# A hybrid decoder layer on one core: transposed memory and norm vectors, a reordered start, value projections inside the cross attention, moved sums

## The chip, the core and the metric

The kernel runs on one core of a Trainium2 chip. The core has a matrix engine (TensorE, PE in the profile), a vector engine (VectorE, DVE), a scalar engine (ScalarE, ACT), a general engine (GpSimd, POOL) and a sync engine (SyncE, SP) that issues most DMAs. Each engine runs its own list of instructions in order, and waits at an instruction until what it reads has been written and what it writes over has been read. TensorE writes to eight PSUM banks; the other engines evict them to SBUF. The metric is the device time of one execution in microseconds (us), as a median of runs.

## The reference

The layer takes x (1024 tokens, 1024 wide) and 256 memory tokens. With h = RMSNorm(x) it computes

```
mq, mk, mv, mi, mf, mo, dq, dk, dv, cq = split(h @ w_in)
y_m = sigmoid(mo) * headnorm(mlstm(conv_silu(mq, mk), mv, mi, mf))   # branch m, 8 chunks of 128
y_d = diff_attention(dq, dk, dv)                                     # branch d, causal
mkv = rms_norm(mem, mem_g) @ w_kv                                    # 512 keys, 1024 values
q   = rms_norm(cq per head); mk = rms_norm(mkv[:512] per head)
y_c = softmax(q @ mk.T / sqrt(128)) @ mkv[512:]                      # branch c, 4 heads
g   = sigmoid(h @ w_gate + b_gate)                                   # three gates
x  += (g_m*(y_m@w_proj_m) + g_d*(y_d@w_proj_d) + g_c*(y_c@w_proj_c)) @ w_out
x  += relu(rms_norm(x) @ w_up)**2 @ w_down
```

All inputs are fp32. The change is in the start, in branch c, and in three short places of the later stages.

## The kernel before, in words

**Arithmetic.** Each fp32 operand is cut into two parts: `split` has ScalarE write a rounded hi part (L124; with a scale per partition L128) and VectorE the rest, lo (L126, L129). Each product is then three matmuls (`mm3`, L96): hi x hi, hi x lo, lo x hi.

**Stages.** (1) `phase_x`: `consts` turns the norm vectors (loaded as 101 rows, `vraw`) into columns (`vec`) by a transpose on TensorE (L222); `mem_kv` transposes the memory (16 transposes, L277) and scales it by the norm's gain into `memT`, projects keys (`wkv[0]`), scales, norms and transposes them (L300 to L310), and projects values (`wkv[1]`, `wkv[2]`); x is normed by rows (ScalarE's Square with a running sum, GpSimd's power, VectorE's product L263) and transposed into `hT` (L101, 64 transposes in 16 groups of four). (2) `branch_c`: the cross attention. A stream of steps of three matmuls (eight query tiles of eight steps, then 64 steps of the sigmoid gates) is woven with items: `turn` (transposes of queries), `scores`, `ptr` (transposes of the softmax), `values`. Each item has the number of a step, behind which it is written. (3) `branch_m`, again a stream with items. Into it `early` puts sums: four blocks of a matrix are loaded (`es`), three or four VectorE sums are made (L1506), and the results are stored for the 7-product scheme that follows later; the sums of y_c go to `xc_d`. (4) The d phase: 32 gate steps with `h_sums` (sums of hT, tiles `hb`, stored to `hc_d`), then projections and attention of branch d. (5) `wino_gates`: the last gate by the 7-product scheme, with operands `hx` read from `hc_d` and split. (6) `branches`, the output projection and `tail` (the MLP), all by the 7-product scheme (`wino`); the inverse norms that the MLP needs are made in `rstd`: sums over partitions by TensorE (`px<-ones,ssq`), a copy `st`, GpSimd's power (L151, L152), a transpose to a row (`px<-ident,st`, L1903), a copy, a store, and a load to all partitions (`rb`).

**Order.** A scheduler places the instructions of a stage on the engines' lists. Where `pinned` is set, TensorE's instructions keep the order in which the code is written; `held` and `issue_after` put an instruction behind a named earlier one.

Of the kernel before, what the change touches and what calls it, by code (L numbers as in the profile page):

```python
# [17 lines left out]
P = 128  # L18
D = 1024
# [54 lines left out]
class Layer:  # L74
# [131 lines left out]
    def consts(self, tmp):  # L206
        nc, cp, a = self.nc, self.cp, self.a
        self.mhalf = cp.tile([P, 32], F32, name="mhalf")
# [13 lines left out]
        nc.tensor.transpose(ps[:, 0:P], raw, self.ident)  # L222
        self.vec = cp.tile([P, P], F32, name="vec")
        nc.vector.tensor_copy(self.vec, ps[:, 0:P])
# [35 lines left out]
    def norm_rows(self, src, r1, scr):  # L260

        self.scale_rows(src, r1, scr)
        self.nc.vector.tensor_scalar_mul(src, src, r1)  # L263

# [5 lines left out]
    def mem_kv(self, pool, tmp, xs, rs):  # L270
        nc, a = self.nc, self.a
        memT = tmp.tile([P, NK, 2, 256], F32R, tag="memT", name="memT")
        for k in range(0, NK, 2):
            ps = self.tp_tile()
            for i in range(2):
                for t in range(2):
                    nc.tensor.transpose(  # L277
                        ps[:, (i * 2 + t) * P : (i * 2 + t + 1) * P], xs[t][:, (k + i) * P : (k + i + 1) * P], self.ident
                    )
            for i in range(2):  # L280
                self.split(
                    memT[:, k + i, 0], memT[:, k + i, 1], ps[:, i * 256 : (i + 1) * 256],
                    self.vec[:, R_MEM + k + i : R_MEM + k + i + 1],
                )
        self.mkT = pool.tile([P, 4, 2, 256], F32R, name="mkT")
        self.mv = pool.tile([P, 2, 2, D], F32R, name="mv")

        def proj(w, t):
            ps = self.mm_tile()
            for k in range(NK):  # L290
                self.mm3(
                    ps, (memT[:, k, 0, t * P : (t + 1) * P], memT[:, k, 1, t * P : (t + 1) * P]), w[k], k == 0, k == NK - 1
                )
            return ps
# [26 lines left out]
    def phase_x(self, kv, tmp):  # L321
# [20 lines left out]
        def half(hf):  # L342
            for x in xs[4 * hf : 4 * hf + 4]:
                norm(x)
# [13 lines left out]
        for _ in gen:  # L358
            pass
# [1939 lines left out]
```

## Time and profile before

| | |
|---|---|
| three runs | 2139.06, 2137.8, 2139.04 us; median 2139.04 us |
| the profiled execution | 2138.05 us, of which the span of the instructions is 2136.2 us; mean granted clock 0.997 |
| TensorE busy | 2106.2 us, 99% |
| VectorE, ScalarE, GpSimd busy | 1559.7, 1058.3, 626.0 us |
| DMA | 335.27 MB, 157 GB/s on average |

The profile is of one execution. A row of waits reads: engine, operation, tile and line of the waiting instruction; after the arrow the engine, tile and line of what came last; then the total, the number of times and the longest. A row of the timeline reads: start, duration, engine, line, operation, what is written and read, shapes, count, and in brackets the idle time before it and who ended it. Rows of overlapping matmuls give an end that is modelled.

### The profile page before, as it was taken

The numbers are of one execution on the slowest core, as the hardware profiler recorded it, in microseconds if no ns is written. First come the engines' busy times: TensorE is split into PE (matmuls) and PEld (weight loads), VectorE is DVE, ScalarE is ACT, GpSimd is POOL, SyncE is SP. The second block draws the span as 40 slices with busy tenths as digits, with TensorE's granted clock in tenths as the row PEclk, the third lists the DMA queues.
The fourth block names the chain that finished last, engine by engine and source line by source line (L and its number), as shares of the span: only waits on it lengthen the run. The fifth ranks groups of instructions, "written<-read, shape, count | busy, mean of one in ns | idle before, by whom it ended". The sixth has DMA issues, their size and how long they took to land.

```text
span 2136.2 us, 31406 instructions
## 1 busy us (share of the span) xinstructions
PE 2106.2 (99%) x10890; PEld 1824.4 (85%) x10890; DVE 1559.7 (73%) x2956; ACT 1058.3 (50%) x2181; POOL 626.0 (29%) x756
## 2 busy tenths in 40 slices
PE   7999999999999999999999999999999999999999
PEld 5888888888899999999888888888788888888887
DVE  6644677787547777777656688975588888777698
ACT  7543365465336666666554445333335544543331
POOL 2100000000111111111023042314756677665562
PEclk9999999999999999999999999999999999999999
DMA  6115457765443333333343885755334544854443
GB/s 233 57 64 167 137 172 223 257 202 182 162 126 91 96 84 85 89 97 89 95 148 119 295 303 161 263 166 174 107 121 173 190 158 156 303 173 135 154 163 109
DMA packets 180789, 335.27 MB, mean 157 GB/s; under 512 B 17385, under 2 KB 52502, under 8 KB 178582
## 3 DMA queue, kind: packets, MB, share of 16 engines
q1 hardware_dynamic: 164694, 307.05, 44.9%
q10 hardware_dynamic: 15936, 26.22, 3.3%
q8 instruction: 86, 1.41, 0.3%
q14 instruction: 73, 0.60, 0.1%
HBM read 213.62 MB, written 94.41 MB: 144 GB/s over the span
## 4 chain that ended last, share of the span: by engine, by line
PE 85%; DVE 5%; DMA 5%; ACT 3%; POOL 1%; issue 1%; SPq 0%; ACTq 0%; DVEq 0%; POOLq 0%
PE mm L96 35%; PE p L96 27%; PE mm L1725 10%; PE sc L96 5%; PE po L96 3%; PE tp L101 3%; DMA ngb<-g_dng 1%; DVE w L126 1%; DMA raw<-in_wkv 1%; PE pr L101 1%; DVE es L1506 1%; DVE cv L686 1%; DMA es<-in_wq 0%; ACT w L124 0%; DMA es<-y 0%
## 5 line engine op out<-in xcount | busy, mean ns | idle before, releaser
L96 PE MATMUL mm<-w,hT 128*128 128x384 f32 (+3 forms) x2496 | 469.4, 331 | 0.8 <-DVE dsg L129 0.7
L96 PE MATMUL mm<-hT,w 128*128 128x512 f32 x1680 | 409.7, 395 | 0.6 <-ACT gt L511 0.6
L96 PEld LDWEIGHTS mm<-w,hT 128*128 128x128 f32 x2496 | 388.7, 189 | 11.7 <-DVE dsg L129 0.9
L96 PEld LDWEIGHTS mm<-hT,w 128*128 128x128 f32 x1680 | 309.4, 189 | 61.3 <-ACT gt L511 1.0
L96 PE MATMUL p<-xo,wo 128*128 128x512 f32 x1344 | 308.4, 392 | 0.0
L96 PE MATMUL p<-xd,wo 128*128 128x512 f32 x1344 | 305.2, 389 | 0.3 <-DVE acc L69 0.3
L96 PEld LDWEIGHTS p<-xo,wo 128*128 128x128 f32 x1344 | 253.8, 189 | 53.6 <-DVE u L69 0.9
L96 PEld LDWEIGHTS p<-xd,wo 128*128 128x128 f32 x1344 | 252.1, 188 | 53.2 <-DVE acc L69 0.7
L117 ACT CAST wo<-wraw 128x896 fp32r<-128x896 f32 x121 | 114.2, 945 | 232.5 <-POOL wraw L1325 88.5
L1725 PE MATMUL mm<-xs,w 128*128 128x512 f32 x1008 | 228.6, 389 | 0.0
L1725 PEld LDWEIGHTS mm<-xs,w 128*128 128x128 f32 x1008 | 189.2, 188 | 39.3
L69 DVE TENSOR_TENSOR wo<-wraw,wo 128x896 fp32r<-128x896 f32 x124 | 150.5, 1224 | 49.1 <-ACT wo L117 49.1
L1322 POOL TENSOR_TENSOR wraw<-wraw 128x128 f32<-128x128 f32 x128 | 101.9, 796 | 196.9 <-DMA wraw<-in_wdown 99.6
L1055 ACT ACTIVATE dpe<-sc,dst,drr 128x256 f32<-128x256 f32 (+7 forms) x128 | 106.6, 833 | 96.9 <-DVE dst L1051 96.4
L126 DVE TENSOR_TENSOR w<-raw,w 128x256 fp32r<-128x256 f32 (+4 forms) x257 | 128.2, 525 | 33.4 <-ACT w L124 32.3
L124 ACT CAST w<-raw 128x256 fp32r<-128x256 f32 (+4 forms) x257 | 116.7, 488 | 41.6 <-PE mm L96 15.0
L151 POOL TENSOR_SCALAR hss<-hss 128x4 f32<-128x4 f32 x8 | 6.2, 774 | 415.0 <-ACT mscr L795 415.0
L1047 DVE CUSTOM_DVE_ANT_0 sc<-sc,tmask 128x256 f32<-128x256 f32 (+7 forms) x128 | 97.1, 759 | 13.4 <-PE sc L96 12.6
L1324 POOL TENSOR_TENSOR wraw<-wraw 128x128 f32<-128x128 f32 x128 | 95.3, 744 | 0.0
L151 POOL TENSOR_SCALAR drr<-drr 128x16 f32<-128x16 f32 x16 | 3.3, 204 | 309.6 <-DVE drr L1002 290.6
L96 PE MATMUL sc<-dk,dq 128*128 128x512 f32 (+3 forms) x384 | 91.9, 347 | 0.0
L1325 POOL TENSOR_TENSOR wraw<-wraw 128x128 f32<-128x128 f32 x128 | 88.0, 687 | 9.9
(330 smaller groups left out, 3456.5 us busy)
## 6 DMA issues: line engine op xcount, KB each, us to landing
dk<-dsg SPq DMA_DIRECT2D x64, 256.0 KB, 4.2
wraw<-in_wup SPq DMA_DIRECT2D x64, 256.0 KB, 3.2
r_d<-xts SPq DMA_DIRECT2D x16, 1024.0 KB, 4.7
wraw<-in_wdown SPq DMA_DIRECT2D x64, 256.0 KB, 3.0
wh<-es SPq DMA_DIRECT2D x56, 256.0 KB, 2.5
w<-wh SPq DMA_DIRECT2D x28, 512.0 KB, 4.3
raw<-in_wd SPq DMA_DIRECT2D x32, 384.0 KB, 3.3
gl<-gates SPq DMA_DIRECT2D x48, 256.0 KB, 4.4
```

Source lines behind the costliest of these rows:

```text
L69: return self.tc.keep_in_program_order(f(*a, **k))
L96: ins = self.nc.tensor.matmul(out, l, r, start=start, stop=stop)
L101: self.pin(self.nc.tensor.transpose(out, x, self.ident))
L117: self.cast = self.A.copy(hi, src).ins
L124: a = nc.scalar.copy(hi, src)
L126: return a, nc.vector.tensor_sub(lo, src, f32(hi))
L1047: V.tensor_tensor_reduce(out=sc[:, 0:n], in0=sc[:, 0:n], in1=self.tmask[:, D - n : D], scale=1.0, scalar=-3.0e38, op0=ALU.add, op1=ALU.max ...
L1055: nc.scalar.activation(pe[c][:, 0:n], sc[:, 0:n], AF.Exp, bias=t8[:, 2 + c : 3 + c], scale=rr[:, i, c : c + 1], accum_out=t8[:, 4 + c : 5 ...
L1322: G.tensor_add(r[:, 4], r[:, 0], r[:, 3])
L1324: G.tensor_sub(r[:, 6], r[:, 1], r[:, 0])
L1325: G.tensor_sub(r[:, 7], r[:, 2], r[:, 5])
L1725: nc.tensor.matmul(cur[u], w[:, l, c], x[:, m], start=first and i == 0, stop=last and i == 2, skip_group_check=True)
```

## The change

The host lays out the norm vectors (`vecs`) and the memory (`memT`) transposed. `vec` is loaded as it is (128 rows of 404 bytes), and the memory's split reads the loaded tile. The memory is still loaded untransposed as well, for its row norms.

`phase_x` is pinned and written anew: keys first, weight piece by weight piece and for both token tiles; then query tiles 0 and 1 woven with the transposes of x; the norms of the second half of x, the rows' norm of the memory and the key norm behind them (the keys are scaled after projection); query tiles 2 and 3 woven with the second half's transposes. In `branch_c` the stream is query tiles 4 to 7 (32 steps), the value projections (32 steps) and 64 gate steps; the value weights are loaded and split in eight pieces (`cut`) inside it. The items have other step numbers, and the pool of the softmax tiles 5 buffers for 8.

In `early` the sums of y_c for the last two of four block pairs are gone; `h_sums` makes them from whole rows (`hb`) in the d phase. In `wino_gates` the second half of the first operand's split (q = 4) is held behind the first evictions. In `wino` the table of places at which `first` takes its next step (here `rstd`'s) changes.

```diff
 def consts(self, tmp):
+        self.vec = cp.tile([P, P], F32, name="vec")
+        nc.sync.dma_start(self.vec[:, 0:R_END], a["vecs"])
...
-        raw = tmp.tile([P, P], F32, tag="vraw", name="vraw")
-        nc.vector.memset(raw, 0.0)
-        nc.sync.dma_start(raw[0:R_END, :], a["vecs"])
-        ps = self.tp_tile()
-        nc.tensor.transpose(ps[:, 0:P], raw, self.ident)
-        self.vec = cp.tile([P, P], F32, name="vec")
-        nc.vector.tensor_copy(self.vec, ps[:, 0:P])
...
 def phase_x(self, kv, tmp):
+        for i in range(4):
+            nc.sync.dma_start(memr[:, 2 * i : 2 * i + 2], a["memT"][:, 2 * i : 2 * i + 2])
+            raws.append(self.w_load(a["wkv"][0], i))
+        xs = [load(a["x"][t * P : (t + 1) * P, :], "xk") for t in range(4)]
+        rawq = [self.w_load(a["wcq"], i) for i in range(4)]
+        xs += [load(a["x"][t * P : (t + 1) * P, :], "xk") for t in range(4, NT)]
         mem = [load(a["mem"][t * P : (t + 1) * P, :], "mx") for t in range(2)]
...
+        for i in range(4):
+            for k in (2 * i, 2 * i + 1):
+                self.split(memT[:, k, 0], memT[:, k, 1], memr[:, k], self.vec[:, R_MEM + k : R_MEM + k + 1])
+            self.w_split(w, raws[i])
+            if i == 3:
+                for x in xs[:4]:
+                    norm(x)
+            for k in (2 * i, 2 * i + 1):
+                for t in range(2):
+                    s = slice(t * P, (t + 1) * P)
+                    self.mm3(ps[t], (memT[:, k, 0, s], memT[:, k, 1, s]), w[k], k == 0, k == NK - 1)
+                if k > 5:
+                    half(0, k - 6)
...
+        for k in range(NK):
+            for t in range(2):
+                self.q_step(ps[t], wq, t, k)
+            if k < 4:
+                half(0, 4 + k)
+            if k % 2 == 1 and k < 7:
+                self.w_split(wq, rawq[k // 2 + 1])
...
 def branch_c(self, pool, w, kv):
+            for t in range(4, NT):
                 ps = self.mm_tile()
                 for k in range(NK):
+                    self.q_step(ps, w, t, k)
+                    if t == 7 and k % 2:
+                        cut()
...
+            for g in (1, 2):
+                for t in range(2):
+                    ps = self.mm_tile()
+                    for k in range(NK):
+                        self.mm3(ps, (self.memT[:, k, 0, s], self.memT[:, k, 1, s]), wv[g][k], k == 0, k == NK - 1)
+                        if g == 1 and t == 1 and k % 2:
+                            cut()
...
 def early(...):
-        S += [([self.y_quad(2, i, kp) for i in range(4)], self.xc[:, kp], True) for kp in range(4)]
+        S += [([self.y_quad(2, i, kp) for i in range(4)], self.xc[:, kp], True) for kp in range(2)]
...
-                sums(p + 17, 7, 9, *S.pop(0))
+                if n < 5:
+                    sums(p + 17, 7, 9, *S.pop(0))
...
 def h_sums(self, pool):
+        for kp in (2, 3):
+            for k in range(2):
+                nc.sync.dma_start(x[-1][k], self.yd[2][2 * kp + k])
+        for kp in (2, 3):
+            V.tensor_sub(r2, r2, r0)
+            V.tensor_sub(r0, r0, r1)
+            V.tensor_add(r1, r2, r1)
+            V.tensor_sub(r3, r3, r1)
+            for i, o in enumerate((r0, r1, r2, r3)):
+                nc.sync.dma_start(self.xc[i, kp], o)
...
 def wino_gates(self, base):
-                if q == 4:
+                if q != 4:
+                    cuts.append(cut)
+                elif i == 0:
                     cut()
                 else:
-                    cuts.append(cut)
+                    with self.held():
+                        cut()
...
 def wino(...):
-                    if (r, kp, j) in ((0, 1, 4), (1, 1, 3), (1, 2, 0), (1, 2, 5)):
+                    if (r, kp, j) in ((0, 1, 4), (1, 2, 4), (1, 3, 0), (1, 3, 4)):
                         first(bank(7))
```

How the lists of the engines change at three places follows. First ScalarE in the start, before: the Squares of x (`scr,r<-xk`), the casts of hT, of key and value weights (`w`) and of the values (`mv`).

```order
L300 ACTIVATE kr_264<-mm_239,r_6_131 128x512
L302 ACTIVATE scr_266<-mm_239,r_6_131 128x512
L267 ACTIVATE scr_320,r_46_319<-xk_303 128x1024
L267 ACTIVATE scr_326,r_48_325<-xk_305 128x1024
L267 ACTIVATE scr_332,r_50_331<-xk_307 128x1024
L124 CAST mkT<-tp_276 128x4x128
L267 ACTIVATE scr_338,r_52_337<-xk_309 128x1024
L128 ACTIVATE mv<-mm_405,r_4_126 128x512
L267 ACTIVATE scr_480,r_68_479<-xk_311 128x1024
L128 ACTIVATE hT<-sc_343,vec 128x512
L128 ACTIVATE hT<-sc_356,vec 128x512
```

ScalarE in the start, now, from the cast of the first query weights on; `mx` is the memory.

```order
L128 ACTIVATE hT<-sc_282,vec 128x512
L124 CAST w_368<-raw_150 128x1024
L257 ACTIVATE scr_386,r_43_385<-xk_152 128x1024
L128 ACTIVATE hT<-sc_282,vec 128x512
L257 ACTIVATE scr_392,r_45_391<-xk_154 128x1024
L257 ACTIVATE scr_398,r_47_397<-xk_156 128x1024
L128 ACTIVATE hT<-sc_306,vec 128x512
L257 ACTIVATE scr_404,r_49_403<-xk_158 128x1024
L257 ACTIVATE scr_409,dv<-mx_160 128x1024
L128 ACTIVATE hT<-sc_306,vec 128x512
L257 ACTIVATE scr_413,dv<-mx_162 128x1024
L128 ACTIVATE hT<-sc_334,vec 128x512
```

The casts of the first half's hT, which the query tiles read, now stand between the Squares of the second half of x and of the memory.

Second, VectorE in branch m at the copy of the state C, before:

```order
L1506 TENSOR_TENSOR es_5441<-es_5441,es_5440 128x512
L736 TENSOR_TENSOR ngb_5866<-ngb_5866,tmaskT 128x512
L1506 TENSOR_TENSOR es_5545<-es_5494,es_5493 128x512
L1506 TENSOR_TENSOR es_5493<-es_5493,es_5492 128x512
L1506 TENSOR_TENSOR es_5494<-es_5494,es_5493 128x512
L781 COPY C_5581<-sc_5574 128x258
L1506 TENSOR_TENSOR es_5495<-es_5495,es_5494 128x512
L126 TENSOR_TENSOR Ch_5583<-C_5581,Ch_5583 128x258
```

and now:

```order
L1581 TENSOR_TENSOR es_5388<-es_5388,es_5387 128x512
L792 TENSOR_TENSOR ngb_5796<-ngb_5796,tmaskT 128x512
L837 COPY C_5511<-sc_5504 128x258
L126 TENSOR_TENSOR Ch_5513<-C_5511,Ch_5513 128x258
L847 TENSOR_TENSOR den_5516<-den_5516,g_col 128x1
```

Four sums that stood around the copy are gone from there.

Third, VectorE at the beginning of the d phase, where `hb` are the sums, `drr` the sums of squares of a tile of branch d and `dv` its values, before:

```order
L126 TENSOR_TENSOR w_6814<-raw_6717,w_6814 128x384
L1175 TENSOR_TENSOR hb_6453<-hT 128x1024
L1182 TENSOR_TENSOR hb_6453<-hb_6453,hb_6445 128x512
L1183 TENSOR_TENSOR hb_6453<-hb_6453 128x512
L1002 TENSOR_REDUCE drr_6522<-dscr_6550 128x4
L126 TENSOR_TENSOR dv_6552<-mm_6523,dv_6552 128x128
```

and now:

```order
L126 TENSOR_TENSOR w_6768<-raw_6671,w_6768 128x384
L1251 TENSOR_TENSOR hb_6467<-hb_6467,hb_6466 128x512
L1252 TENSOR_TENSOR hb_6466<-hb_6466 128x512
L1254 TENSOR_TENSOR hb_6466<-hb_6467,hb_6466 128x512
L1058 TENSOR_REDUCE drr_6452<-dscr_6484 128x4
L126 TENSOR_TENSOR dv_6486<-mm_6453,dv_6486 128x128
L1255 TENSOR_TENSOR hb_6467<-hb_6467,hb_6466 128x512
```

Three of the four sums of y_c that the d phase now makes from the tile hb_6467 and its neighbour stand ahead of the first tile's reduction and values.

In `tail`, on TensorE's list the transpose `px<-ident,st` stood 39 matmuls behind `px<-ones,ssq`, and stands 63 behind it now. ScalarE's and GpSimd's lists keep their order there; on VectorE's the lo part of the rest of the fourth operand X[3] (`xo<-xts`) moves ahead of two lo parts of weights (`wo`).

More of the change, by code (lines that the diff above doesn't have):

```diff
@@ L321, in phase_x, with q_norm @@
+    def q_norm(self, qr, r4, scr):
+        self.nc.scalar.activation(scr, qr, AF.Square)
+        self.nc.vector.tensor_reduce(r4, scr.rearrange("p (h d) -> p h d", h=4), axis=AX.X, op=ALU.add)
+        self.rsqrt_mean(r4, r4, 128, 4)
     def phase_x(self, kv, tmp):
@@ L328, in load @@
             return x
-        def norm(x, tag="r1", rows=self.norm_rows):
-            r = tmp.tile([P, 1], F32, tag=tag, name=self.name("r1"))
-            scr = tmp.tile([P, D], F32, tag="sq", name=self.name("scr"))
-            rows(x, r, scr)
-            return r
-        mem = [load(a["mem"][t * P : (t + 1) * P, :], "mx") for t in range(2)]
-        self.consts(tmp)
-        gen = self.mem_kv(kv, tmp, mem, [norm(x, "rm", self.scale_rows) for x in mem])
-        next(gen)
-        xs = [load(a["x"][t * P : (t + 1) * P, :], "xk") for t in range(NT)]
@@ new lines, in phase_x @@
+        kr = tmp.tile([P, 2, 512], F32, tag="kr", name="kr")
+        for t in range(2):
+            nc.scalar.copy(kr[:, t], ps[t])
+        half(0, 2)
+        self.w_split(wq, rawq[0])
+        half(0, 3)
+        ps = [self.tp_tile() for _ in range(2)]
+        for k in range(NK):
[5 more added lines that the diff above has]
+                self.w_split(wq, rawq[k // 2 + 1])
@@ new lines, in phase_x @@
+        for t in range(2):
+            nc.scalar.copy(self.Q[t][0], ps[t])
+        for x in xs[4:]:
+            norm(x)
+        rs = [self.dv[:, 38 + t : 39 + t] for t in range(2)]
+        for t in range(2):
+            self.scale_rows(mem[t], rs[t], scratch())
+        self.rs = rs
+        kr4 = tmp.tile([P, 8], F32, tag="kr4", name="kr4")
+        for t in range(2):
+            nc.vector.tensor_scalar_mul(kr[:, t], kr[:, t], rs[t])
+            r4 = kr4[:, 4 * t : 4 * t + 4]
+            self.q_norm(kr[:, t], r4, scratch()[:, 0:512])
+            k4 = kr[:, t].rearrange("p (h d) -> p h d", h=4)
+            nc.vector.tensor_mul(k4, k4, r4.unsqueeze(2).broadcast_to([P, 4, P]))
@@ L368, in branch_c, with fetch, cut @@
         self.pinned = True
-        w = self.load_w(a["wcq"], 512, 2)
-        Q, pr, pT = {}, {}, {}
+        Q, pr, pT = self.Q, {}, {}
+        r8 = pool.tile([P, 32], F32, tag="cr4", name="cr8")
+        src = [(g, i) for g in (1, 2) for i in range(4)]
+        wv, raws = {1: [], 2: []}, []
+        def fetch():
+            if src:
+                g, i = src.pop(0)
+                raws.append((g, self.w_load(a["wkv"][g], i)))
+        def cut():
+            g, raw = raws.pop(0)
+            self.w_split(wv[g], raw)
+            fetch()
@@ L2245, in pack @@
     w["mem"] = i["mem"][0]
+    w["memT"] = i["mem"][0].T.reshape(8, P, 256).transpose(1, 0, 2)
     kv = i["w_mem_kv"][0]
```

175 lines of the change are left out of this document (88 added, 87 removed).

## The prediction

> **What bounds the kernel now.** First the page's busy time, then the waits of TensorE, then the windows in which a wait stands.
>
> ```profile
> span 2136.2 us, 31406 instructions
> PE 2106.2 (99%) x10890; PEld 1824.4 (85%) x10890; DVE 1559.7 (73%) x2956; ACT 1058.3 (50%) x2181; POOL 626.0 (29%) x756
> L1725 PE MATMUL mm<-xs,w 128*128 128x512 f32 x1008 | 228.6, 389 | 0.0
> ...
> PE tp L222 <- DMA vraw<-in_vecs: 8.0, 1, 8.0
> PE px L1903 <- POOL st L152: 4.2, 1, 4.2
> PE sc L96 <- ACT Ch L124: 3.1, 3, 2.2
> ```
>
> TensorE is busy 99% of the span, so only work taken from TensorE or a wait of TensorE can move the time. The group of line 1725 is a stretch without gaps: 228.6 us for 1008 matmuls, 0.2268 us each, the price of one 128x512 matmul below. The waits (total, times, longest) name the places: the start, one C state of branch m, and the row of inverse norms before the MLP.
>
> ```profile
> 30.00:40.00 10.00, 7.73 (x37) 5.42 (x36) 7.06 (x15) 7.73 (x14) 5.64 (x11) 1.00 0.69 271
> 60.00:70.00 10.00, 10.00 (x54) 8.34 (x53) 8.20 (x13) 6.62 (x13) 0.62 (x2) 1.00 0.18 52
> 510.00:520.00 10.00, 10.00 (x51) 8.57 (x51) 7.61 (x19) 7.90 (x25) 0.00 (x0) 0.85 0.26 72
> 1530.00:1540.00 10.00, 5.81 (x18) 4.34 (x17) 8.36 (x8) 2.01 (x3) 9.68 (x11) 0.68 0.25 69
> ```
>
> Columns: window, length, busy PE, PEld, DVE, ACT, POOL, granted clock, DMA share, GB/s. After each of the two later waits the clock stands below 1: a wait costs its own length and then half speed for a while.
>
> **A. The start.** The change takes 17 transposes from TensorE (16 of the memory, 1 of the vectors) and puts the same 144 matmuls and 72 other transposes in another order. Where both kernels have done those is read here:
>
> ```profile
> 12.42 3.62 PE L96 MATMUL mm<-w,memT 128*128 128x512 f32 x10
> 47.26 0.44 PE sc L101 x4
> 59.90 0.86 PE L96 MATMUL mm<-w,hT 128*128 128x512 f32 x3
> ```
>
> Four transposes take about 0.45 us. At 59.90 the 144 matmuls that read memT are done and four groups of x transposes are left, so the common work ends at 59.9 + 4x0.45 = 61.7 us. It is 144x0.2268 + 18x0.45 = 40.8 us of work; the 17 transposes are 1.9 us; the other 19 us are waiting and a slow first stretch (ten matmuls took 3.62 us, not 2.27).
>
> Now the new order. Rows for its steps:
>
> ```profile
> 0.71 1.28 ACT L267 ACT_TABLE_LOAD   x1 [0.71 <-PEq L2288]
> 4.38 1.06 ACT L267 ACTIVATE scr<-mx 128x1024 f32<-128x1024 f32 x1 [2.38 <-DMA mx<-in_mem]
> 9.10 1.04 ACT L124 CAST w<-raw 128x1024 fp32r<-128x1024 f32 x1 [2.12 <-DMA raw<-in_wkv]
> 10.34 1.04 ACT L124 CAST w<-raw 128x1024 fp32r<-128x1024 f32 x1 [0.20 <-DMA raw<-in_wkv]
> 31.03 1.07 ACT L267 ACTIVATE scr<-xk 128x1024 f32<-128x1024 f32 x1
> 32.22 1.06 ACT L267 ACTIVATE scr<-xk 128x1024 f32<-128x1024 f32 x1
> 33.94 0.33 PE L101 MATMUL sc<-ident,xk 128*128 128x128 f32 x1 [0.45 <-DVE xk L263]
> L128 ACT ACTIVATE hT<-sc,vec 128x512 fp32r<-128x512 f32 x16 | 10.3, 689 | 2.8 <-PE sc L101 2.8
> L126 DVE TENSOR_TENSOR w<-raw,w 128x1024 fp32r<-128x1024 f32 x16 | 19.4, 1219 | 13.3 <-ACT w L124 13.3
> 26.99 1.01 POOL L152 TENSOR_TENSOR r<-r,mhalf 128x4 f32<-128x4 f32 x1
> ```
>
> The first 512 KB (mx) are in at 4.3 us, the third at about 9.1, the fourth 1.25 later. The first weight piece now comes behind 0.3 MB instead of 1.1, so at about 6.1 (an estimate between the times of the second and the third 512 KB, 5.3 to 6.8). ScalarE's table load (1.28) now stands behind the first memory piece, at about 4.4, and two memory casts follow it, so the cast of the weights (1.04) begins at 6.6 and the first matmul at 7.7 (7.0 to 8.4). From that weight piece to the fourth x tile come 8.5 loads of 512 KB; at 1.35 us each, a little over the 1.25 seen, it is there at 17.6. From a Square's start to the first transpose it was 33.94 - 31.03 = 2.9 us, so the first x transposes end at 21.0. From there ScalarE sets the pace, in the order that front shows: eight hT casts (0.69, 5.5), three weight casts (3.1), two key copies (1.2, an estimate from the rows of 128x512), six Squares at 1.19 from start to start (7.1), two half Squares (1.3): 18.2 us, and with 0.2 of small waits 39.4. The last lo part waits on VectorE behind the key norm (POOL's 1.01 us row, a reduction, a product): some 2.7 more, 42.1, and the last four matmuls of tiles 0 and 1 end at 43.0. Tile 2 with seven transpose groups takes 24x0.2268 + 7x0.45 = 8.6, the last group, the key transposes and tile 3 another 1.35 + 5.45: 58.4. So the start gains 61.7 - 58.4 = **3.3 us**, of which 1.9 are the transposes and only 1.4 waiting. Bounds: 2 and 4 by the landing; 0 if ScalarE is held more. I take 3.1. Two waits leave (line 222's 8.0 becomes 7.7), two new ones come (hT casts behind Squares of the other x tiles).
>
> The pieces of value weights that now run between query tiles cost ScalarE 1.04 and VectorE 1.22 each: 2.3 us from the time that a slot comes free, and TensorE reads the piece six steps of three matmuls (4.1 us) later. With 1.8 us in hand I price them at nothing, and at up to 1.2 us a piece if VectorE is full there.
>
> **B. The sums taken from branch m.** TensorE waits for the C state:
>
> ```profile
> 504.13 0.69 DVE L736 TENSOR_TENSOR ngb<-ngb,tmaskT 128x512 f32<-128x512 f32 x1 [2.48 <-DMA ngb<-g_dng]
> 505.40 2.14 DVE L1506 TENSOR_TENSOR es<-es,es 128x512 f32<-128x512 f32 x3 [0.57 <-DMA xc_d<-es]
> 507.46 0.42 DVE L781 COPY C<-sc 128x258 f32<-128x258 f32 x1
> 505.66 0.52 PE L96 MATMUL sc<-va,mpT 128*128 128x258 f32 x3
> 508.37 1.01 PE L96 MATMUL sc<-Ch,qp 128*128 128x258 f32 x3 [2.19 <-ACT Ch L124]
> ```
>
> Three es sums, late themselves for a DMA, stand ahead of the copy C. Without them the copy starts when ngb is done (504.8), C is there at 505.25, its cast some 0.45 later at 505.7, its lo part at 506.2; TensorE comes at 506.18. So about 2.0 of the 2.19 go. The half clock behind it goes too: 10 us at 0.85 is 1.5 us, and it began a little before 510, 0.2 more. **3.7 us**, between 2.0 (the clock falls anyway) and 3.9. The Trainium skill (TensorE: Matmul & The Clock Gate, Part 1) puts the fall of the clock to a whole idle window of about 3.4 us; by it this 2.2 us wait costs only itself and the term is 2.0. The trace disagrees: the clock is 0.85 right behind the wait.
>
> **C. Where those sums go.** Eight VectorE sums of 0.69, four loads of 512 KB and eight stores now stand in the d phase's beginning, on VectorE ahead of the eviction of a dv tile:
>
> ```profile
> L1185 SPq DMA_DIRECT2D hc_d<-hb x8: 319/326/327, 566.7 to 593.4; - x8
> DMA to landing us min/median/max: 2.6/2.6/5.1
> 592.75 13.57 PE L96 MATMUL mm<-w,hT 128*128 128x384 f32 x77
> 597.86 0.42 DVE L1002 TENSOR_REDUCE drr<-dscr 128x4 f32<-128x256 f32 x1 [4.52 <-ACT dscr L998]
> 602.02 0.42 DVE L1002 TENSOR_REDUCE drr<-dscr 128x4 f32<-128x256 f32 x1 [3.54 <-ACT dscr L998]
> ```
>
> The last store of hb goes out at 593.4 and frees its buffer at 596.0; the load into it lands 3.3 to 4 later, 599.5; three sums follow, 601.6, then the reduction and dv, 602.3. Tiles follow each other every 4.16 us (602.02 - 597.86) from 592.75, with two banks: the third tile needs the bank at 601.07. **Loss 1.2 us**, between 0 (the load is quicker by that) and 3.
>
> **D. The gate's first eviction.** One cast of 1.04 and its subtraction go behind it:
>
> ```profile
> 1121.84 0.68 ACT L511 ACTIVATE gt<-mm,dv 128x512 f32<-128x512 f32 x1
> 1122.57 3.06 PE L96 MATMUL mm<-hT,w 128*128 128x512 f32 x12 [0.56 <-ACT gt L511]
> ```
>
> That cast has the shape of the weights' (1.04), and the activation comes this much sooner, more than TensorE's wait: **0.6 us** gained. The held half now comes after the activations; its cast and subtraction end about 2.9 us after the first of them, at 1124.4, before the 3.06 us of matmuls that stand ahead of its use are done (1125.1), so nothing is late for it. If it were, the gain would be gone: 0 to 0.6.
>
> **E. The row of inverse norms.** Its transpose moves 24 matmuls (5.4 us) later, more than the 4.19 that it waited:
>
> ```profile
> 1522.02 9.15 PE L96 MATMUL p<-xo,wo 128*128 128x512 f32 x39
> 1535.36 0.38 PE L1903 MATMUL px<-ident,st 128*8 128x128 f32 x1 [4.19 <-POOL st L152]
> 1539.66 0.94 ACT L117 CAST wo<-wraw 128x896 fp32r<-128x896 f32 x1 [7.11 <-POOL wraw L1325]
> 1540.50 1.91 ACT L124 CAST xo<-xts 128x2048 fp32r<-128x2048 f32 x1
> 1542.44 2.29 DVE L126 TENSOR_TENSOR xo<-xts,xo 128x2048 fp32r<-128x2048 f32 x1 [0.62 <-ACT xo L124]
> ```
>
> What is late next is the rest of X[3]. TensorE, done with the 39 at 1531.2, needs 30 more and two of X[3]'s products, and is there at 1539.3 without the wait; ScalarE's cast of the rest ends at 1542.41, because it is queued behind a weight cast that waits for POOL's sums, whose order does not change. VectorE's lo part ends at 1544.73. So TensorE waits 3.2 + 2.1 us there, in place of 4.19. Before, at 1544.73, TensorE (at half speed until about 1540.5, by the 0.68) stood at the first product of X[3]; now it is seven or eight matmuls further, 1.7 us, and pays the half clock after the new wait, 0.9 to 2.5. **Nothing**, between a gain of 1.5 and a loss of 1.
>
> **The sum.** -3.1 - 3.7 + 1.2 - 0.6 + 0 = -6.2 us. The profiled execution took 2138.05 (span 2136.2 and 1.85 around it), 1 us under the median of the runs, 2139.04. Forecast: **2131.8 us**. About 0.2%, 4.3 us, is what a measurement here can tell from no change.
>
> **Rivals.** *The px wait is gone for good* (chance 0.17): X[3]'s rest comes earlier, since POOL's sums run to TensorE's pace and ScalarE was idle 7.11 us before. Then 4.19 and 2.6 us of half clock go (6.8 us at half speed by the 0.68 and a little of the next window, 1.7 of it idle, so 5.1/2): 2131.8 - 6.8 = 2125. Against it: POOL is 9.68 busy of 10 there, so nothing moves its last sum forward. *The start gains nothing* (0.17): ScalarE, busy 7.73 of 10 in the window at 30 before, now has the Squares between the hT casts; each handoff from ScalarE to VectorE to TensorE that I count at nothing costs some 0.4 us, and eight of them take the 3.1 back: 2134.9, no change that can be told. Against it: before, ScalarE had idle time there, so its work alone does not fill it. *Slower* (0.10): the value pieces bind VectorE. Eight subtractions of 1.2 us come in two stretches of about 7.4 us each, four in each, beside the softmax; where VectorE has under 4.9 us free in a stretch, all of a piece's 1.2 lands on TensorE: 8x1.2 = 9.8, and two windows of half clock, 1.7 each: -6.2 + 13.2 = +7, 2145. It decides from the point where the wait at a piece is over 0.5 us; for it speaks that VectorE is busy 8.20 of 10 in the window at 60 without the pieces, against it the 1.8 us in hand.
>
> **How the numbers follow.** Forecast 0.50, the three rivals 0.17, 0.17, 0.10, small other mixtures 0.06. Alone the forecast's own range is 2129 to 2135, from the bounds of A, B, C and E taken half each. The range that holds 8 in 10 reaches to the px rival and to the start's: 2124.5 to 2137.5. Faster by over 0.2%: 0.50 + 0.17 + some of the rest, 0.71; within: 0.19; slower: 0.10.
>
> **What would show it.** A: the first matmul between 7.0 and 8.4, first x transposes at about 20.5, the common work done at 58 to 59. B: no wait on Ch, clock 1.00 in the windows at 510. C: a wait for dv or drr of about 1.2 us near 595 to 600. D: no wait on gt. E: no px wait, but one on xo of 3 us and one of 2, with a clock below 1 behind it. Wrong it would be made by a wait in the cross attention (on w, mv or cqT), or by no xo wait at all.

## The result and the profile after

The changed kernel is slower: runs of 2153.01, 2155.82 and 2157.05 us, where the kernel before took 2138.65 us (median of 2137.8 to 2139.06) beside it; the ratio is 1.0081, with an interval of 1.0067 to 1.0095. (A fourth execution took 7915.81 us, unlike all others, and is not in the ratio.) 2131.8 us had been predicted, with 2124.5 to 2137.5 as the range. The profiled execution took 2157.05 us, with a span of 2155.3, 19.1 us more than before.

The head of the page, then TensorE's waits in the changed kernel (what waited and for whom, total, times, longest):

```profile
span 2155.3 us, 31366 instructions
PE 2110.7 (98%) x10873; PEld 1827.4 (85%) x10873; DVE 1560.4 (72%) x2950; ACT 1059.0 (49%) x2181; POOL 620.9 (29%) x756
```

```profile
PE sc L101 <- DVE hT L129: 9.4, 8, 3.7
PE mm L96 <- ACT w L124: 9.2, 2, 8.0
PE mm L96 <- ACT gt L567: 6.5, 3, 3.1
PE sc L96 <- DVE cqT L129: 2.9, 3, 1.3
PE p L96 <- DVE xo L126: 2.4, 1, 2.4
PE p L96 <- ACT xo L124: 2.2, 1, 2.2
PE sc L96 <- ACT cqT L128: 2.1, 2, 1.3
```

The old waits are gone: px, and the 2.2 us on Ch (1.2 us are left on that tile, 1.0 at most at once). Of the 9.2 us on w, 8.0 are the wait of the first matmul. In their place stand waits on hT in the start, on cqT in the cross attention, on gt in two places, and the two on xo that were foretold. The windows of the changed kernel (length, busy PE, PEld, DVE, ACT, POOL, granted clock, DMA share, GB/s) show half speed behind several of them, and full speed where branch m had stood at 0.85:

```profile
30.00:40.00 10.00, 8.81 (x36) 6.56 (x35) 6.77 (x13) 8.69 (x16) 5.11 (x11) 0.82 0.41 164
100.00:110.00 10.00, 10.00 (x49) 8.32 (x49) 6.69 (x13) 5.68 (x14) 1.20 (x2) 0.90 0.37 125
510.00:520.00 10.00, 10.00 (x52) 8.51 (x51) 5.50 (x12) 2.73 (x9) 0.00 (x0) 1.00 0.38 132
610.00:620.00 10.00, 10.00 (x49) 10.00 (x49) 3.73 (x8) 1.33 (x5) 0.00 (x0) 0.80 0.39 150
1560.00:1570.00 10.00, 8.39 (x28) 6.77 (x29) 9.48 (x12) 0.95 (x1) 4.34 (x8) 0.69 0.18 52
```

**A ledger by stage.** Four instructions stand at the border of a stage in every kernel, so their start times split the span. In the timeline of TensorE before:

```profile
194.53 20.68 PE L96 MATMUL mm<-w,hT 128*128 128x264 f32 x169
570.08 1.03 PE L101 MATMUL tp<-ident,hS 128*128 128x128 f32 x8
708.31 0.60 PE L101 MATMUL tp<-ident,doS 128*128 128x128 f32 x4
1125.47 11.07 PE L96 MATMUL mm<-hx,w 128*128 128x512 f32 x48
```

and after:

```profile
208.43 6.82 PE L96 MATMUL mm<-w,hT 128*128 128x264 f32 x51 [1.13 <-ACT w L124]
577.89 1.03 PE L101 MATMUL tp<-ident,hS 128*128 128x128 f32 x8
721.02 0.60 PE L101 MATMUL tp<-ident,doS 128*128 128x128 f32 x4
1142.83 7.52 PE L96 MATMUL mm<-hx,w 128*128 128x512 f32 x32
```

These are branch m's first matmul, its end, a point 138 us into the d phase, and the first product of the last gate. The end of the start is the 144th matmul along the timeline: 61.7 before (as in the prediction, with the transposes), 66.7 after. The stages of the change against before: start +5.0, cross attention (208.43 - 66.7 less 194.53 - 61.7) +8.9, branch m -6.1, beginning of the d phase +4.9, rest of it and the gates +4.7, output projection and MLP +1.7; together 19.1.

### The profile page after: what moved, and what is told of

The parts are those of the page before. It is cut to its first block, busy times and chain, and to the rows that moved or that the text cites. A ratio compares the mean times of both kernels' runs of the same rounds, so it can differ in the third digit from the quotient of the medians.

```text
span 2155.3 us, 31366 instructions
## 1 busy us (share of the span) xinstructions
PE 2110.7 (98%) x10873; PEld 1827.4 (85%) x10873; DVE 1560.4 (72%) x2950; ACT 1059.0 (49%) x2181; POOL 620.9 (29%) x756
## 4 chain that ended last, share of the span: by engine, by line
PE 82%; DVE 5%; DMA 4%; ACT 3%; POOL 2%; issue 2%; SPq 0%; DVEq 0%; POOLq 0%; ACTq 0%
PE mm L96 36%; PE p L96 23%; PE mm L1801 11%; PE sc L96 6%; PE po L96 3%; PE tp L101 3%; DMA ngb<-g_dng 1%; PE pr L101 1%; DVE w L126 1%; DVE acc L69 1%; PE tp L96 1%; DMA es<-in_wq 1%; DMA raw<-in_wd 0%; DMA xk<-in_x 0%; DMA xd<-r_d 0%
## 5 line engine op out<-in xcount | busy, mean ns | idle before, releaser
L96 PE MATMUL mm<-w,hT 128*128 128x384 f32 (+3 forms) x2448 | 459.9, 331 | 4.3 <-ACT gt L567 3.1
L96 PEld LDWEIGHTS mm<-w,hT 128*128 128x128 f32 x2448 | 382.8, 190 | 13.5 <-ACT gt L567 3.4
```

The costliest lines, as they stand in the source:

```text
L96: ins = self.nc.tensor.matmul(out, l, r, start=start, stop=stop)
```

## Where the waits come from

**The start.** The timeline of TensorE in the changed kernel, and one row of VectorE:

```profile
20.54 0.50 PE L101 MATMUL sc<-ident,xk 128*128 128x128 f32 x3
...
28.83 1.12 PE L101 MATMUL sc<-ident,xk 128*128 128x128 f32 x4 [3.66 <-DVE hT L129]
...
46.34 0.84 PE L96 MATMUL mm<-w,hT 128*128 128x512 f32 x3
47.02 0.60 PE L101 MATMUL sc<-ident,xk 128*128 128x128 f32 x4
47.38 0.94 PE L96 MATMUL mm<-w,hT 128*128 128x512 f32 x3
49.68 0.66 PE L101 MATMUL sc<-ident,xk 128*128 128x128 f32 x4 [1.37 <-DVE hT L129]
```

```profile
48.88 0.74 DVE L129 SCALAR_TENSOR_TENSOR hT<-sc,vec,hT 128x512 fp32r<-128x512 f32 x1
```

An sc tile holds the transposes of two k (`half`: k % 2). Those of the second k wait until the lo part of the first has been read from the tile: VectorE's row begins at 48.88 and takes 0.74, so it ends at 49.62, and the transposes start at 49.68. The two k lie in different halves of the tile, but the wait is for the tile. Every second k so pays a whole round of transposes, ScalarE's hi part and VectorE's lo part, and TensorE's own order lets only three matmuls run meanwhile.

**The cross attention.** ScalarE, VectorE and TensorE of the changed kernel around the first pair of waits:

```profile
93.41 2.00 ACT L124 CAST w<-raw 128x1024 fp32r<-128x1024 f32 x2
95.31 0.69 ACT L128 ACTIVATE cqT<-tp,dv 128x512 fp32r<-128x512 f32 x1
```

```profile
94.83 2.35 DVE L126 TENSOR_TENSOR w<-raw,w 128x1024 fp32r<-128x1024 f32 x2
97.10 0.74 DVE L129 SCALAR_TENSOR_TENSOR cqT<-tp,dv,cqT 128x512 fp32r<-128x512 f32 x1
```

```profile
96.05 0.50 PE L96 MATMUL sc<-mkT,cqT 128*128 128x256 f32 x2 [0.73 <-ACT cqT L128]
97.89 2.03 PE L96 MATMUL sc<-mkT,cqT 128*128 128x256 f32 x10 [1.35 <-DVE cqT L129]
```

Two casts of value weights, which nobody needs yet, are queued ahead of the queries that TensorE needs now, on both engines. A second pair (1.33 and 0.97 us near 150) has four exponentials ahead of cqT.

**The beginning of the d phase.** SyncE, ScalarE and TensorE of the changed kernel:

```profile
599.70 1.77 SPq L1241 DMA_DIRECT2D hc_d<-hb  x2
601.57 0.41 SPq L1008 DMA_DIRECT2D raw<-in_wd  x1
602.92 1.89 SPq L1247 DMA_DIRECT2D hb<-y  x2
604.90 1.08 SPq L1008 DMA_DIRECT2D raw<-in_wd  x2
```

```profile
607.11 0.51 ACT L124 CAST w<-raw 128x384 fp32r<-128x384 f32 x1 [6.04 <-DMA raw<-in_wd]
607.53 0.68 ACT L567 ACTIVATE gt<-mm,dv 128x512 f32<-128x512 f32 x1
```

```profile
608.26 17.43 PE L96 MATMUL mm<-w,hT 128*128 128x384 f32 x84 [3.09 <-ACT gt L567]
```

A cast waits on ScalarE for a load of weights (6.04 us), behind the cast a gate's eviction, and TensorE waits for the bank. The load is the one that SyncE issues at 601.57: it lands 5.5 us later, when the cast starts. It is the fourth of its kind behind branch m. In the kernel before, the fourth goes out at 582.69, 12.6 us behind branch m's end, and takes 5.1 us; here it goes out 23.7 us behind it. So it is issued late, and hardly slower in landing. On SyncE's list it now stands behind four stores of the moved sums and the stores of hb, and these wait for the sums: SyncE stood waiting for 3.4 us before the store at 599.70. Those of the moved loads of y_c that wait for buffers (`hb<-y`, 602.92) stand behind this load, not ahead of it.

## The experiments

The kernel before took 2136.41, 2135.87 and 2136.75 us (medians) beside the three groups of runs. Profiled stages, as differences from the kernel before in us:

| run | median us | ratio to before | start | cross att. | branch m | d, begin | d, gates | rest |
|---|---|---|---|---|---|---|---|---|
| the change, first | 2155.82 | 1.0081 | +5.0 | +8.9 | -6.1 | +4.9 | +4.7 | +1.7 |
| after_again | 2151.03 | 1.0073 | +3.8 | +8.9 | -6.0 | +2.5 | +1.5 | +1.0 |
| two_tiles | 2144.13 | 1.0042 | -1.9 | +7.5 | -5.0 | +1.5 | +1.4 | -0.2 |
| late_sums | 2148.44 | 1.0055 | +4.1 | +8.8 | -4.0 | -0.8 | +3.1 | +0.5 |
| px_back | 2149.28 | 1.0065 | +5.0 | +8.9 | -5.2 | +1.4 | +1.6 | -0.8 |
| items | 2147.55 | 1.0054 | +4.3 | +4.8 | -4.5 | +2.7 | +1.3 | +0.3 |
| hold_back | 2151.13 | 1.0066 | +4.0 | +8.9 | -5.9 | +4.9 | +2.7 | +1.3 |
| start_free | 2141.68 | 1.0024 | -4.6 | +10.1 | -5.2 | +4.4 | +0.8 | -1.9 |
| all4 | 2137.24 | 1.0009 | -2.2 | +5.0 | -4.6 | -1.2 | +2.6 | +0.3 |
| all5 | 2133.94 | 0.9991 | -4.4 | +5.1 | -7.3 | -1.3 | +1.7 | -0.2 |
| b_late | 2132.62 | 0.9980 | together | +0.9 | -6.7 | -0.5 | +0.4 | +1.0 |
| b_sums | 2137.75 | 1.0008 | together | +0.1 | -6.5 | +5.5 | +0.7 | -1.7 |
| b_rest | 2138.69 | 1.0012 | together | +0.7 | -6.8 | +4.3 | +1.7 | +1.1 |

The column "rest" is 1010.7 us long and moves by -1.9 to +1.7 with either wino table: differences of that size are not read there.

### after_again: the changed kernel itself, once more

No edit.

> The changed kernel once more, unchanged, for a second profile. Theory 1 (order of the lists): the waits that stand against the kernel before, 4.8 us in the start, 9.2 in the cross attention, 5.0 at the beginning of the d phase, come back to within 0.5 us each, and 6.5 us are again gained in branch m; the time is 2153 to 2158. Theory 2 (chance of a transfer): the wait of TensorE on gt at the last gate (1.2 and 2.2 us in the first profile, behind a load of fr that took 7.7 us to land where 3.8 is the median) is not there again, or is under 1 us, and the time is about 4 us lower than in the first profile, 2151 to 2153. If the fr load takes over 6 us again, it is no chance.

2151.03 us (2149.87 to 2155.45), 1.0073 [1.0057, 1.0089]. The start and the cross attention cost what they did; the d phase and the gates 5.5 us less together. TensorE's waits on gt sum to 4.1 us, not 6.5, and in these two stages the clock stood at half speed for 3.4 us, not 10.2 (the last section says when it does). So some 5 us of the first profile's loss was the chance of when loads land and how the waits met the clock, and the rest belongs to the change.

### two_tiles: two sc tiles in turn

```diff
-            if k % 2 == 0:
-                self.hsc = self.sc_tile()
-            ps = self.hsc[:, k % 2 * 512 : k % 2 * 512 + 512]
+            if k % 4 == 0:
+                self.hsc = [self.sc_tile() for _ in range(2)]
+            ps = self.hsc[k % 2][:, k // 2 % 2 * 512 : k // 2 % 2 * 512 + 512]
```

> The changed kernel with one edit: the transposes of x for four k go in turn to two PSUM tiles, so that the second half of a tile is written two k after the first instead of right behind it. Theory 1: a transpose into the second half of a tile waits until both engines have read the first half (eight waits, 9.4 us in all, four of them 0.86 to 1.37 us in query tile 2). With two k between, those four go and the ones in tiles 0 and 1 shrink: the start ends 4 to 6 us sooner, the whole is 4 to 6 us faster than the changed kernel. Theory 2 (rival: ScalarE is full in the start and sets its end whatever the tiles): the waits move to w or hT and under 1.5 us is gained.

2144.13 us, 1.0042 [1.0028, 1.0057]: 6.9 us less than after_again. The eight waits on hT became two (1.98 and 2.61), and branch m started at 200.15 instead of 207.21. Each k still has its half; only which tile the next k shares has changed. So it was the tile, and neither the evictions' length nor the landings.

### start_free: the order of the start left to the scheduler

```diff
 def phase_x(self, kv, tmp):
-        self.pinned = True
```

> The changed kernel with the order of the start left to the scheduler, as the kernel before has it, and not pinned to the order of the code; every instruction and every tile as in the change. In the built order two sc tiles then take turns for the eight k, and matmuls of the query tiles 2 and 3 move ahead of those of tiles 0 and 1. Theory 1: the loss of the start is the pinned order, in which each second half of an sc tile waits until both readers of its first half are done: the eight waits on hT (9.4 us) fall to two at most, branch m starts 5 to 8 us earlier than in the changed kernel (207.2 us), as it did with two sc tiles in turn (200.15), and the time is 2143 to 2146. Rival: the waits come from the eviction's length (0.74 us on VectorE, 0.6 us on ScalarE, for every k) and the norms ahead of it, in whatever order: branch m starts within 2 us of 207 and the time is 2149 to 2152.

2141.68 us (2138.36 to 2143.24), 1.0024 [1.0014, 1.0033]: 9.4 below after_again. Branch m starts at 200.01, 7.2 earlier; the rest of the 9.4 comes later and was not traced. In TensorE's list the two tiles of a pair now take turns, and matmuls of query tiles 2 and 3 (mm_55, mm_62) stand between those of 0 and 1 (tp_36, tp_37):

```
30 L96 MATMUL mm_55_432<-w_35_289,hT_75 128x512
31 L96 MATMUL tp_36_298<-w_35_289,hT_75 128x512
32 L96 MATMUL tp_37_299<-w_35_289,hT_75 128x512
33 L96 MATMUL mm_55_432<-w_35_289,hT_75 128x512
34 L96 MATMUL mm_62_524<-w_35_289,hT_75 128x512
35 L101 MATMUL sc_33_260<-ident_106,xk_5_136 128x128
```

The 144th matmul is done at 57.1. That is near the end that the prediction had for the start (58.4), by another order of matmuls than the one that it walked through. The new layout does win 4.6 us, when nothing pins TensorE to wait for a tile, and no half clock stands in this start behind its first 13 us. The two waits of the transposes on hT sum to 2.1 us; two more of the query matmuls, on ScalarE's hi part and VectorE's lo part, are 1.7 and 0.4. The longest by VectorE was this:

```profile
43.91 0.66 PE L101 MATMUL sc<-ident,xk 128*128 128x128 f32 x4 [1.44 <-DVE hT L129]
```

### items: another order in the cross attention

```diff
-            p = 8 * t + 4 if t < 5 else 51 + 4 * t
+            p = (4, 12, 20, 33, 37, 71, 75, 79)[t]
             add(p, turn, t)
-            add(p + (3 if t < 5 else 2), scores, t)
+            add(p + 3, scores, t)
```

> The changed kernel with another order of the items of the cross attention: turns at items 4, 12, 20, 33, 37, 71, 75, 79 and each turn's scores always three items behind it, so that the casts of the value weights do not stand ahead of the last turns' casts. Theory 1: the 9.15 us that the cross attention lost are mostly TensorE waiting for cqT (0.73, 1.35, 1.33, 0.97 us) behind w casts and exponentials, and the half clock after two of them (1.7 us): these four waits leave the list of the cross attention, the granted clock between 90 and 110 us stays at 1.0, and branch m's first matmul starts 4 to 6 us earlier than in the changed kernel (207.2 us in its second run); in all about 2146. Rival: the loss comes with the pieces as such (the value and query matmuls cut into more pieces, at whatever place): the waits go, but branch m starts less than 2 us earlier, and the time stays at 2150 to 2153.

2147.55 us, 1.0054 [1.0039, 1.0069], 3.5 less than after_again, and branch m starts 3.6 us earlier. The pair at 96 is gone and the clock stays at 1.00 there; of the other pair one wait remains:

```profile
154.72 1.45 PE L96 MATMUL sc<-mkT,cqT 128*128 128x256 f32 x10 [0.97 <-DVE cqT L129]
...
203.58 11.67 PE L96 MATMUL mm<-w,hT 128*128 128x264 f32 x91 [1.13 <-ACT w L124]
```

Theory 1 holds a little short of its 4 to 6. The cross attention is still 4.8 us longer than before: 3.5 of that are listed waits (0.97 and 1.13 above, and four others of 0.29, 0.38, 0.51 and 0.17); the rest was not traced to a cause.

### late_sums, and the sums alone: b_sums and b_late

The moved sums over x of y_c, with their loads and stores, are put behind a marked matmul of the d phase, in the changed kernel (late_sums) and in the kernel before with nothing but the moved sums (b_late; b_sums has these moved as the change has them):

```diff
+        def late(ins):
+            self.behind(ins.ins, self.mark)
...
-                nc.sync.dma_start(x[-1][k], self.yd[2][2 * kp + k])
+                late(nc.sync.dma_start(x[-1][k], self.yd[2][2 * kp + k]))
...
-            V.tensor_sub(r2, r2, r0)
+            late(V.tensor_sub(r2, r2, r0))
...
-                nc.sync.dma_start(self.xc[i, kp], o)
+                late(nc.sync.dma_start(self.xc[i, kp], o))
```

> The changed kernel with one edit: the loads, sums and stores of y_c in the d phase are put behind the matmul after which they are written, which lets the weight loads raw<-in_wd of the first two heads go ahead of the loads hb<-y on SyncE's list. Theory 1: the 3.1 us wait on gt at the beginning of the d phase comes from ScalarE standing at a weight cast whose raw load was issued behind hb<-y, which waits for a store; with the raw loads ahead the wait goes and so does the half clock behind it: 4 to 5 us faster than the changed kernel. Theory 2 (rival, the prediction's: VectorE stands at the sums ahead of dv): the sums are still close to the first dv on VectorE's list, so 0 to 2 us only, and a wait on dv or drr shows.

2148.44 us, 1.0055 [1.004, 1.007]: the fourth load of weights goes out at 591.52, again 12.6 us behind branch m's end. There is no wait of TensorE between 590 and 620 us any more, and the d phase's beginning is 3.3 us shorter than in after_again. So theory 1 had the right list, but not what stands in the way on it: the edit holds back loads, sums and stores together, and by the trace above it is the stores that stood ahead of this load. The time fell by only 2.6: branch m won 1.9 less in this execution and the gates lost 1.6 more.

> The kernel before, with only the sums moved into branch m, as in the change, and with the sums over x of y_c (third and fourth) with their loads and stores put behind the marked matmul of the d phase; start, cross attention, the gates' hold and the wino table are as before. Theory 1 (the parts add up): branch m wins the 6.5 us that it won in the changed kernel (or the 3.7 that were foretold), and the d phase loses nothing, as it did with the late sums in the changed kernel: 4 to 6 us faster than the kernel before, about 2131 to 2133. Rival: branch m's gain came from starting with the queues in another state after the new cross attention, and without that the wait for the state at 510 us stays: within 1.5 us of the kernel before.

2132.62 us (2130.32 to 2133.87), 0.9980 [0.9971, 0.9989]: faster than both kernels. Branch m wins its 6.7 us behind the old start and cross attention too, so it owes nothing to them.

```profile
564.33 1.03 PE L101 MATMUL tp<-ident,hS 128*128 128x128 f32 x8
```

(570.08 before.) The median shows 3.3 of the 6.7; in the profiled execution the gates and the rest took 1.4 back.

> The kernel before with only the sums moved into branch m, the sums over x not held back to the marked matmul (the run b_late had them held back and came out at 2132.62). Theory 1: the d phase's loss belongs to the moved loads alone, which stand ahead of the raw loads on SyncE, so it comes without the new start and cross attention too: branch m's last transposes start at about 564.3, 5.8 us earlier than in the kernel before, TensorE waits 2 to 3 us on gt near 595, and the time is 1.5 to 3 us above b_late's, 2134 to 2135.5. Rival: that wait needs the queues as the new cross attention leaves them: no wait on gt, and the same time as b_late, 2132 to 2133.5.

2137.75 us, 1.0008 [0.9998, 1.0017]: by the medians 5.1 us more than b_late (some 4 with each taken from the kernel before in its own group), beyond the 1.5 to 3 expected, and no better than before. The wait comes with the moved sums, their loads and stores alone:

```profile
594.41 16.80 PE L96 MATMUL mm<-w,hT 128*128 128x384 f32 x84 [2.87 <-ACT gt L511]
```

and the clock stood at 0.73 in the 5 us around it. Here too the late load (588.14) is issued ahead of the `hb<-y` that wait for buffers (589.11). What branch m wins, the d phase loses, 6.5 against 5.5: that the loss needs no new start and cross attention holds, that the loads make it does not, and the price is above what was expected.

### px_back, hold_back and b_rest: the table and the hold

```diff
-                    if (r, kp, j) in ((0, 1, 4), (1, 2, 4), (1, 3, 0), (1, 3, 4)):
+                    if (r, kp, j) in ((0, 1, 4), (1, 1, 3), (1, 2, 0), (1, 2, 5)):
```

> The changed kernel with the table of places in wino as before, so that the transpose of the inverse norms is 24 matmuls earlier again. Prediction's term E: no difference, -1.5 to +1 us, with the 4.2 us wait on st back in place of the two waits on xo (2.2 and 2.4 us). Rival: the table gains what the wait on st cost, and undoing it costs 3 us or more.

2149.28 us, 1.0065 [1.005, 1.008]: the 4.2 us on px is back, the two waits on xo are gone, and the time is 1.8 below after_again with overlapping ranges. The table is worth nothing that can be told.

In hold_back the hold of the change is undone:

```diff
-                if q != 4:
-                    cuts.append(cut)
-                elif i == 0:
+                if q == 4:
                     cut()
                 else:
-                    with self.held():
-                        cut()
+                    cuts.append(cut)
```

> The changed kernel with the hold of the hx cast in the Winograd gates taken back to what it was. Theory 1: the hold moves one cast behind the gate's, and another takes its place ahead, so that the order ahead of the second gt is as long as before: the wait of some 2.2 us on gt near 1133 stays, and the time is within 1 us of the changed kernel's 2151. Rival: the hold itself made the wait (TensorE stood with no such wait there in the kernel before): the wait goes and the stage is 2 to 4 us shorter.

2151.13 us, 1.0066 [1.0047, 1.0085], the changed kernel's time; TensorE waited 0.73 and 2.25 us on gt. That is theory 1: three casts of hx stand between the two gates' evictions on ScalarE's list in the kernel before, in the change and here. What the wait goes with is a load. GpSimd, in the change's first profile, waits for the last of three early pairs of weight loads (before, it did not):

```profile
1129.59 0.74 POOL L1279 TENSOR_TENSOR fr<-fr 128x256 f32<-128x256 f32 x1 [3.32 <-DMA fr<-in_wgq]
```

ScalarE's casts and then gt stand behind these sums. The last of these six loads took 4.0 us to land in the kernel before, and TensorE's waits on gt there sum to 0.56. With the old hold it took 4.9, 5.2, 7.1 and 7.2, and the waits sum to 1.03, 1.28, 2.98 and 2.94 (b_late, b_sums, hold_back, all4). With the new hold it took 5.4, 5.9, 6.1 and 7.7, and they sum to 1.46, 1.94, 2.16 and 3.45 (start_free, two_tiles, after_again, the first profile). The two series run into each other, so the hold itself is worth nothing that can be told. One run stands apart: in b_rest this load took 4.0 and the wait is 2.27, but two casts of hx ahead of gt waited 1.10 and 0.61 for loads of their own. Why the loads land later in some kernels stays open.

b_rest is the kernel before with the moved sums, this hold and this table, as the diff of the change has them.

> The kernel before with all of the change except its start and its cross attention: the moved sums, the hold in the gates and the wino table. Theory 1: the change's whole loss sits ahead of branch m (12.7 us in the changed kernel's second run), and of the rest the sums win 6.6, give 2 to 3 back in the d phase, and hold and table are worth nothing within 1.5 us: 2132.5 to 2136, level with or below the kernel before. Rival: hold and table cost too (the gt waits of 2.2 us come with the hold, and two xo waits with the table): 2137 to 2140, not below the kernel before.

2138.69 us, 1.0012 [1.0002, 1.0022]. That is in the rival's range, but so is b_sums (2137.75), on which theory 1's range had been built too low: the moved sums give back more in the d phase than was thought. Above b_sums it is 0.9 us, and the intervals overlap: what hold and table cost together cannot be told from nothing. Start and cross attention are as before here and branch m begins 0.7 us late, against 12.7 in after_again: that difference is the start and the cross attention of the change.

### all4 and all5: the repairs together

all4 is two_tiles, items, late_sums and hold_back in one; all5 is start_free, items and late_sums.

> The changed kernel with two sc tiles in turn at the start, the other order of the items in the cross attention, the late sums over x, and the gates' hold as before. Theory 1: the repairs add up, 6.9 (start) and 4 to 6 (items) and 2.6 (late sums) and 0 (hold) below the changed kernel's 2151: about 2135.5 to 2137.5, level with the kernel before. Rival: what one stage wins the next gives back in a wait for a landing that does not come earlier: 2141 to 2144, no better than the two tiles alone.

2137.24 us, 1.0009 [0.9999, 1.0018]: inside 2135.5 to 2137.5. The repairs add up.

> The changed kernel with the start's order left to the scheduler, the other order of the items in the cross attention, and the late sums over x. Theory 1: the repairs add up as they did with two tiles in turn (2137.24): 2135 to 2139. If the scheduler's start is better than two tiles in turn, because tiles 2 and 3 fill what waits are left (1.98 and 2.60 us there), 2131 to 2135, level with the kernel before with the late sums alone (2132.62). Rival: the scheduler moves casts ahead of those that the cross attention waits for, and the waits on cqT come back: 2139 to 2143.

2133.94 us, 0.9991 [0.9981, 1.0000]; in the profiled execution (span 2129.8) branch m begins only 0.7 us late and ends 6.6 early. With the free start it is 3.3 us under all4. The ranges of b_late and all5 overlap; b_late stands 0.2% below the kernel before, all5 0.1%, with an interval that reaches 1.

## Why the prediction was wrong, point by point

**A, the start.** Foretold -3.1, came out at +5.0 and +3.8. The first matmul (8.03, in the 7.0 to 8.4) and the first x transposes (20.54, about 20.5) were right. The step that failed is "From there ScalarE sets the pace": eight hT casts cannot follow each other, since every second one waits for transposes that wait for VectorE's reading of the tile's other half. Tiles 0 and 1 ended at 46.3, not 43.0, and "Tile 2 with seven transpose groups takes 24x0.2268 + 7x0.45 = 8.6" took 12.4 (46.34 to 58.8), of which 3.1 are three waits; a fourth of 0.87 follows. The order of ScalarE quoted ahead of the prediction shows hT casts in pairs from one sc tile (sc_282, sc_306); that TensorE writes the second half only when VectorE, too, has read the first was not asked. The half clock behind the longest wait, 3.66 us, has no term in the sum either: two steps of 3.41 us in the first profile, one in after_again. The rival on the start came nearest: it had eight handoffs at some 0.4 us each, and the eight waits on hT sum to 9.4. With the scheduler's order the start ends at 57.1, near the 58.4, but by another order, so that this does not bear out the single terms.

**The value pieces and the items' order.** Foretold 0, came out at +8.9 for the cross attention. The step that failed is "With 1.8 us in hand I price them at nothing". The hand was that of the piece; a cast also holds up what is queued behind it, and cqT has no slack: 0.73 and 1.35 us of waiting and one step of half clock, up to 1.7. The new order of the items has no term in the prediction at all; the second pair, 1.33 and 0.97, stands behind exponentials, and with the items at other places the 1.33 went. With 1.13 on branch m's first weights that is 7.2 of the 8.9; the rest was not traced. Moving the items took back 4.1. The slower rival named the right stage and the right sign, by another mechanism: TensorE never waited for a piece there, and VectorE was not full.

**B, branch m.** Foretold -3.7, came out at -4.0 to -7.3, -6.7 with the old stages around it. The mechanism is right: the wait on Ch (2.19) and the half clock behind it (1.7) went as foretold, 3.9 together. The size was too small. All waits of the stage sum to 4.6 before and 1.4 in b_late, so 1.0 of smaller waits went too; the remaining 1.8 were not traced.

**C, the d phase.** Foretold +1.2 by way of VectorE's sums; came out at +1.4 to +5.5 where these are not held back. The step that failed is "The last store of hb goes out at 593.4 and frees its buffer at 596.0; the load into it lands 3.3 to 4 later": it followed the moved work to VectorE and its dv tile only. On SyncE's list the moved stores stand ahead of weight loads, and the fourth of these, 11 us later than before, held up ScalarE's cast, the gate behind it, and TensorE for 3.09 us (1.97 in after_again). The wait on dv that was foretold is real too: it came in two runs behind that on gt, with 1.70 (b_rest) and 1.62 us (start_free).

**D, the gates.** Foretold -0.6; the hold came out at nothing, in a stage that lost 0.8 to 4.7 with the new hold and 0.4 to 2.7 with the old one. The step that failed is "One cast of 1.04 and its subtraction go behind it": that is true, but another operand's cast takes the free place ahead of the eviction, and the changed list has as many as the old one. What the stage lost on gt goes with a late load.

**E, the table.** Foretold 0 with waits of 3.2 and 2.1 on xo, clock below 1 behind them: came out at 0 within the spread of some 2 us, with 2.18 and 2.43 and 0.69. This was right, and its rival, the wait gone for good, did not come.

## What to carry to other kernels

When an order is pinned, ask of every tile with two halves who still reads the first half when the second is written: the wait is for the tile, and a scheduler that put two tiles in turn had hidden it. A moved cast or store is to be priced by what stands behind it on its engine's list, not by when its own result is needed; here stores that had to wait for sums belonged behind loads that need not wait. Where several moves come in one change, their stages can be told apart by the start times of a few landmark instructions, and the good part (here the sums, held back) taken alone.

## What the runs showed of the clock

Waits of about the same length, at the same place, sometimes cost half speed and sometimes nothing. Windows of 3.41 us with TensorE's busy time, granted clock, DMA share and GB/s, and the wait, in after_again:

```profile
602.59:606.00 3.41, 1.44 (x9) 1.00 0.97 341
606.00:609.41 3.41, 3.41 (x12) 0.50 1.01 337
...
605.81 16.40 PE L96 MATMUL mm<-w,hT 128*128 128x384 f32 x84 [1.97 <-ACT gt L567]
```

and in px_back:

```profile
604.28:607.69 3.41, 1.75 (x11) 1.00 0.95 347
607.69:611.10 3.41, 3.12 (x18) 1.00 0.98 351
...
607.98 15.18 PE L96 MATMUL mm<-w,hT 128*128 128x384 f32 x84 [1.95 <-ACT gt L567]
```

The windows are not chosen freely. In each of the 14 profiles every change of the granted clock lies a whole number of steps of 3.413 us behind the first change, to within 2 ns, and half speed lasts one step or two. In after_again the wait of 1.97 us lies inside one step, and the next step runs at 0.50. In px_back a step ends within the wait of 1.95, which leaves 1.66 us of idle time in one and 0.29 in the next, and the clock stays. Outside the last 60 us of each profile, 39 steps at full speed were followed by half speed, and TensorE was idle for at least 1.64 us in each; in the 8364 that were followed by full speed it was idle for at most 1.77. So by these profiles what decides is whether about half of a step is idle, and with that where a wait falls: 2.17 us (items) brought half speed, while 2.47 (b_rest) and 2.72 (start_free) were cut by the end of a step and did not.

A step at half speed loses up to 1.7 us; the 84 matmuls behind the two waits took 16.40 and 15.18 us, 1.2 apart. So a wait of 2 us costs 2, or up to nearly 4. The first profile of the change has eight such steps, after_again four, the kernel before three; the prediction took half clock as certain behind each wait.

The Trainium skill (TensorE: Matmul & The Clock Gate, Part 1) says that the activity window of the clock gate is free-running, so that the same kernel meets it at another phase each time. The steps agree with that, and their length with its some 3.4 us. Its rule that the clock falls after an idle window does not hold here: about half a window of idle time sufficed.
